# A two-layer network on one core: dummy products, a parameter load and operand casts are placed otherwise

## The chip, the cores and the metric

The kernel runs on one core of a Trainium2 chip. The core has a tensor engine (PE, with its weight loads listed apart as PEld), VectorE (DVE), ScalarE (ACT), GpSimd (POOL) and SyncE (SP), whose queue issues almost all transfers. The metric is the device time of one execution in microseconds (us); three executions before the change took 2072.78, 2072.91 and 2074.65 us, median 2072.91.

## The reference

Two layers on 1024 tokens of 1024 features, float32 throughout. Layer 0 mixes tokens by attention in a sliding window of 128 with a sink, layer 1 by a gated recurrence (HGRN2) in chunks of 64; each is followed by an MLP with a squared ReLU, and every block is preceded by an RMS norm.

```python
for layer in range(DEPTH):
    h = rmsnorm(x, mix_norm[layer])
    y = attention(h, ...) if layer % 2 == 0 else hgrn2_recurrence(h, ...)
    x = x + y
    h = rmsnorm(x, mlp_norm[layer])
    x = x + jnp.square(jax.nn.relu(h @ w_up[layer])) @ w_down[layer]
return rmsnorm(x, final_norm)
```

`rmsnorm` multiplies by the reciprocal root of the mean square over the features and by a gain per feature.

## The kernel before

**Layout.** Activations lie with 128 features on the partitions and 512 tokens along a tile, so a full activation is eight tiles for each of two token halves (`hf`). The program is written as Python code that names operations, their tiles and their costs; it issues nothing itself.

**Products in three parts.** A float32 operand is split in two reduced-precision tiles: `hi`, a cast of it, and `lo`, the operand less `hi`. A product is then three: hi by hi, hi by lo, lo by hi (`mm3`). Weights come from memory into `wr` tiles (or are sums of such tiles, `m`), and `weight_split` makes `wh` and `wl`; for activations `split` does the same. The cast could be placed on ScalarE or on VectorE, whichever suited the plan; the subtraction is always VectorE's. Most large products are arranged after Strassen with seven leaves in place of eight, and three of the leaves of the MLP's up projection again in quarters; of the tile called "4" in those inner leaves only the right half (columns 256 to 511) is read by a product. `pair` makes two of the up projection's 32 blocks of features at a time, 16 pairs a layer; PE accumulates several leaves one after the other in the same bank, and ScalarE copies the bank out between them.

**Order.** All operations go to one planner (`Schedule`). It runs a list of them forward with estimated costs, the engines' queues and buffer releases, and backward for due times, in four passes, and keeps the pass with the earliest end. From this come the order on every engine, the engine of those operations that may choose, and the buffers. At run time each engine works through its own list in that order and waits by semaphores. A changed cost or choice can therefore move instructions anywhere in the program. Line 428 is the helper that issues every operation, so the profile names tiles and not lines: `p` and `q` are banks of the accumulation memory, `a`, `t` and `m` are work tiles, `c` constants, `sm` the few numbers of a norm, `d` memory for tiles put by.

**Start.** `Net.__init__` makes ten products of a zero tile with itself (`warm`), to have the tensor engine active while the first loads come. `first_loads` loads the parameters (gains and lower bounds, 16 rows) by SP's queue, transposes them with four small products into the constant tile `c`, and loads the first activations and weights.

**End.** The down projection's last sum for token half 1 is computed in two parts of 256 tokens. `final` is called three times: for half 0, for the first 256 tokens of half 1, and for the last 256. Each call adds the squares of all features (`sum_squares`), takes the mean over the partitions by products with a column of 1/1024 (`token_rstd`, in two portions, since the last tile of features is finished late), forms the reciprocal root, spreads it over the partitions by products with the identity (`spread`), and multiplies and stores. Between and behind the portions `token_rstd` puts products of the identity with itself, four and five of them, in all three calls. The two calls on 256 tokens spread twice, into two banks, one read by VectorE and one copied by ScalarE for GpSimd.

Of the kernel before, what the change touches and what calls it, by code (L numbers as in the profile page):

```python
# [10 lines left out]
F32 = mybir.dt.float32  # L11
# [3 lines left out]
ALU = mybir.AluOpType  # L15
AX = mybir.AxisListType

P = 128
# [4 lines left out]
TH = T // NH  # L23
# [3 lines left out]
N_PAR = 8 * KT  # L27
# [113 lines left out]
WAIT = 0.5  # L141
TABLE, REUSE, PASSES = 1283.0, 200.0, 4
FULL = {512: 227.3, 256: 119.8}
LEAD = 100
WARM = 10
ROWS = 16
# [4 lines left out]
class Schedule:  # L151
# [40 lines left out]
    def forward(self):  # L192

        free_at, pending, ready, done, form, table = {}, {}, {}, [], None, None
# [179 lines left out]
class Net:  # L374
# [24 lines left out]
    def warm(self, zero, n=WARM, tag="p"):  # L399

        ps = self.psum(tag)
        for _ in range(n):
            self.mm(ps[:, :P], zero, zero, True, True, P, 4)
# [100 lines left out]
    def weight_split(self, z):  # L504
        hi, lo = (self.tile(tag, BUFS[tag], (P, TH), F32R) for tag in ("wh", "wl"))
        self.copy(hi, z, TH, ("ACT", "DVE"), False)
        self.tt("any", lo, z, hi.bitcast(F32), ALU.subtract)
        return hi, lo
# [12 lines left out]
    def split(self, src, new=None):  # L521
        hi, lo = ((new or self.a)(F32R) for _ in range(2))
        self.copy(hi, src, TH, ("ACT", "DVE"), False)
        self.tt("any", lo, src, hi.bitcast(F32), ALU.subtract)
        return hi, lo
# [18 lines left out]
    def token_rstd(self, acc, inner=1.0, outer=1.0, n=TH, keep=False, more=()):  # L544
# [4 lines left out]
        for i, z in enumerate(parts):  # L549
            for j in range(nb):  # L550
                first, last = (j == 0, j == nb - 1) if more else (True, True)
                self.mm(ps[:, j : j + 1], z[:, j * P : j * P + P], self.mean, i == 0 and first, i == len(parts) - 1 and last, P, 2,
                        skip_group_check=bool(more))
            if more and z is acc:
                self.warm(self.ident, 4, "q")
        if more:
            self.warm(self.ident, 5, "q")
# [140 lines left out]
    def strassen_weights(self, first, second, done=(), inner=()):  # L698
# [29 lines left out]
        w = {name: self.weight_split(z) for name, z in order}  # L728
# [3 lines left out]
    def inner_operands(self, own, kept, homes):  # L732
# [33 lines left out]
        for j, c in enumerate((L, R) if homes else ()):  # L766
            hi, lo = part(own[j], R, "R")
            self.copy(hi, t[0][:, c], 2 * P, ("ACT", "DVE"), False)
# [382 lines left out]
    def first_loads(self):  # L1151
# [5 lines left out]
        self.dma(rows[:ROWS], self.io["par"], 4 * P * N_PAR)  # L1157
# [493 lines left out]
    def final(self, hf, tokens=slice(0, TH)):  # L1651
# [3 lines left out]
        y = self.token_rstd(first, n=n, more=[last])  # L1655
        r, rs = self.spread(y, n), self.t()[:, :n]
        self.copy(rs, self.spread(y, n) if n < TH else r, n)
        self.s.lead = -200
        per = TH // n
        for k in range(0, KT, per):  # L1660
# [4 lines left out]
            step = 1 if n < TH and k == per else per  # L1665
# [98 lines left out]
```

## Time and profile before

| | |
|---|---|
| median of three executions | 2072.91 us |
| the profiled execution in all | 2074.11 us |
| its span (first to last instruction) | 2072.3 us |
| records on PE, DVE, ACT, POOL | 12290, 3870, 2319, 121 |
| moved by DMA | 407.44 MB, 197 GB/s on the mean |

A row of the timeline has the start, the duration of the merged row, the engine, the operation, what it writes and reads, the tile, and the count; in brackets stands the idle time ahead of it and what ended it. A row of groups has the busy time in all, the mean duration in ns, and behind the second bar the idle time of that engine just before, with its releasers. Records of successive products overlap, so a product's cost to the stream is the distance between starts. A float32 product of tiles that aren't split shows two records. A row of the windows has the stretch, its length, and then the busy time of PE, PEld, VectorE, ScalarE and GpSimd with their counts. The chain of work that ended last is followed back from the last instruction; its rows have the start, the length and what held the end.

### The profile page before, as it was taken

What the parts mean: (1) busy time and instruction counts of PE and PEld (TensorE: products, weight loads), DVE (VectorE), ACT (ScalarE), POOL (GpSimd) and SP (SyncE); (2) the same over time, 40 slices, a digit from 0 to 9 for tenths busy, and PEclk for the clock granted to TensorE, in tenths of its full rate; (3) what the DMA queues carried; (4) which work ended last, traced back from release to release, by engine and by line L of the source; (5) the groups of instructions that cost most, each with busy time, mean ns of one, the idle gap of its engine ahead of it and who ended that gap; (6) DMA issues with size and microseconds to landing.
All of it is one profiled execution on the core that took longest, in us unless ns stands there. A gap on an engine that the chain in (4) does not pass through costs nothing.

```text
span 2072.3 us, 35730 instructions
## 1 busy us (share of the span) xinstructions
PE 2062.5 (100%) x12290; PEld 1753.2 (85%) x12290; DVE 1908.8 (92%) x3870; ACT 1139.5 (55%) x2319; POOL 61.1 (3%) x121
## 2 busy tenths in 40 slices
PE   9999999999999999999999999999999999999998
PEld 7888788888898888888888888888888888888888
DVE  8999989999999989999999999889999999998994
ACT  7477966655565434656544544444665556433562
POOL 4121000000000000000000000000000000000000
PEclk9999999999999999999999999999999999999999
DMA  6212468777679887542322223677887677996712
GB/s 220 84 45 77 148 229 277 258 242 249 213 243 311 299 262 262 182 129 72 113 102 98 97 93 102 232 245 240 263 265 262 213 241 262 316 311 218 254 51 82
DMA packets 225766, 407.44 MB, mean 197 GB/s; under 512 B 25248, under 2 KB 30368, under 8 KB 225584
## 3 DMA queue, kind: packets, MB, share of 16 engines
q1 hardware_dynamic: 225584, 405.16, 59.2%
q8 instruction: 97, 1.59, 0.3%
q14 instruction: 85, 0.70, 0.1%
HBM read 321.17 MB, written 83.89 MB: 195 GB/s over the span
## 4 chain that ended last, share of the span: by engine, by line
PE 96%; issue 1%; DMA 1%; DVE 1%; ACT 0%; POOL 0%; POOLq 0%; SPq 0%; ACTq 0%
PE p L428 52%; PE q L428 44%; DMA d<-t 0%; ACT t L428 0%; DMA t<-d 0%; DVE t L428 0%; DMA wr<-in_up 0%; DVE m L428 0%; DVE wl L428 0%; DVE a L428 0%; POOL a L428 0%; ACT wh L428 0%; POOLq L1738 0%; ACT a L428 0%; SPq L428 0%
## 5 line engine op out<-in xcount | busy, mean ns | idle before, releaser
L428 PE MATMUL p<-a,wh 128*128 128x512 f32 (+1 forms) x2880 | 804.4, 364 | 0.0
L428 PE MATMUL q<-a,wh 128*128 128x512 f32 x2112 | 653.2, 391 | 1.4 <-ACT t L428 1.4
L428 PEld LDWEIGHTS p<-a,wh 128*128 128x128 f32 x2880 | 515.5, 189 | 84.5 <-issue 0.4
L428 PE MATMUL p<-a,wl 128*128 128x512 f32 (+1 forms) x1440 | 520.4, 362 | 0.0
L428 PEld LDWEIGHTS q<-a,wh 128*128 128x128 f32 x2112 | 389.4, 188 | 78.3 <-ACT t L428 2.8
L428 PE MATMUL q<-a,wl 128*128 128x512 f32 x1056 | 410.2, 389 | 0.0
L428 PEld LDWEIGHTS p<-a,wl 128*128 128x128 f32 x1440 | 271.6, 189 | 40.1
L428 ACT CAST wh<-wr 128x512 fp32r<-128x512 f32 x285 | 175.9, 621 | 182.1 <-PE p L428 138.5
L428 DVE TENSOR_TENSOR wl<-wr,wh 128x512 fp32r<-128x512 f32 x352 | 240.9, 689 | 9.2 <-ACT wh L428 4.6
L428 ACT CAST wh<-m 128x512 fp32r<-128x512 f32 x262 | 162.2, 621 | 152.0 <-PE q L428 78.8
L428 DVE TENSOR_TENSOR wl<-m,wh 128x512 fp32r<-128x512 f32 x338 | 231.2, 689 | 13.1 <-ACT wh L428 4.6
L428 PEld LDWEIGHTS q<-a,wl 128*128 128x128 f32 x1056 | 198.3, 188 | 42.1
L428 DVE TENSOR_TENSOR a<-t,a 128x512 fp32r<-128x512 f32 (+2 forms) x314 | 208.2, 681 | 5.8 <-PE q L428 2.9
L428 DVE TENSOR_TENSOR t<-t,t 128x512 f32<-128x512 f32 (+3 forms) x337 | 197.5, 603 | 10.0 <-ACT t L428 6.9
L428 ACT ACTIVATE t<-t 128x512 f32<-128x512 f32 x228 | 143.7, 632 | 101.6 <-DVE t L428 97.5
L428 ACT COPY t<-q 128x512 f32<-128x512 f32 (+2 forms) x201 | 111.7, 560 | 110.2 <-PE q L428 87.1
L428 ACT CAST a<-t 128x512 fp32r<-128x512 f32 (+1 forms) x206 | 122.6, 610 | 70.7 <-PE q L428 46.6
L428 PE MATMUL p<-wh,a 128*128 128x512 f32 x384 | 125.9, 398 | 1.1 <-ACT a L428 1.1
L428 DVE TENSOR_TENSOR t<-t,p 128x256 f32<-128x256 f32 x294 | 120.8, 417 | 6.0 <-PE p L428 2.1
L428 DVE TENSOR_TENSOR m<-wr,wr 128x512 f32<-128x512 f32 (+1 forms) x188 | 121.5, 648 | 2.6 <-DMA wr<-in_down 1.9
L428 PEld LDWEIGHTS q<-t,t 128*64 128x64 f32 (+1 forms) x2160 | 95.8, 144 | 12.0 <-issue 8.1
L428 PE MATMUL q<-t,t 128*64 128x32 f32 (+2 forms) x2160 | 104.6, 229 | 0.0
(134 smaller groups left out, 2393.0 us busy)
## 6 DMA issues: line engine op xcount, KB each, us to landing
t<-d SPq DMA_DIRECT2D x548, 256.0 KB, 4.2
d<-t SPq DMA_DIRECT2D x244, 256.0 KB, 3.3
wr<-in_down SPq DMA_DIRECT2D x224, 256.0 KB, 4.1
wr<-in_up SPq DMA_DIRECT2D x178, 256.0 KB, 3.7
wr<-in_win SPq DMA_DIRECT2D x68, 256.0 KB, 2.9
a<-d SPq DMA_DIRECT2D x60, 256.0 KB, 4.0
wr<-in_wqkv SPq DMA_DIRECT2D x48, 256.0 KB, 3.1
d<-a SPq DMA_DIRECT2D x48, 256.0 KB, 3.7
```

Source lines behind the costliest of these rows:

```text
L428: fn(*[place(a) for a in args], **{k: place(v) for k, v in kw.items()})
```

## The change

It does six things.

- Of the ten dummy products at the start the count stays, but their cost in the plan is now 430 ns each; the planner also starts its engines at 700 to 850 ns and not at zero (`FIRST`).
- The parameters are loaded by ScalarE's queue and not by SP's.
- `token_rstd` places dummies in the last of the three final calls alone: three and four of them where it had four and five, with a cost of 217 ns in the plan.
- The second spread is made in the last call alone; in the second call one bank is read by both. A group of features that was stored tile by tile in the second and third call is so in the third alone.
- Every cast of a split runs on ScalarE.
- Of the inner leaves' tile "4" only the half that is read is cast and subtracted.

```diff
+FIRST = {"SP": 700.0, "PE": 850.0, "ACT": 700.0, "DVE": 800.0, "Pool": 800.0}
...
-        free_at, pending, ready, done, form, table = {}, {}, {}, [], None, None
+        free_at, pending, ready, done, form, table = dict(FIRST), {}, {}, [], None, None
...
-    def warm(self, zero, n=WARM, tag="p"):
+    def warm(self, zero, n=WARM, tag="p", cost=430.0):
 
         ps = self.psum(tag)
         for _ in range(n):
-            self.mm(ps[:, :P], zero, zero, True, True, P, 4)
+            self.op("PE", self.nc.tensor.matmul, [ps], [zero], cost, ps[:, :P], zero, zero, start=True, stop=True, form="whole")
...
-    def weight_split(self, z):
+    def weight_split(self, z, first=0):
         hi, lo = (self.tile(tag, BUFS[tag], (P, TH), F32R) for tag in ("wh", "wl"))
-        self.copy(hi, z, TH, ("ACT", "DVE"), False)
-        self.tt("any", lo, z, hi.bitcast(F32), ALU.subtract)
+        c, n = slice(first, TH), TH - first
+        self.copy(hi[:, c], z[:, c], n, psum=False)
+        self.tt("any", lo[:, c], z[:, c], hi[:, c].bitcast(F32), ALU.subtract, n)
         return hi, lo
...
     def split(self, src, new=None):
         hi, lo = ((new or self.a)(F32R) for _ in range(2))
-        self.copy(hi, src, TH, ("ACT", "DVE"), False)
+        self.copy(hi, src, TH, psum=False)
...
-    def token_rstd(self, acc, inner=1.0, outer=1.0, n=TH, keep=False, more=()):
+    def token_rstd(self, acc, inner=1.0, outer=1.0, n=TH, keep=False, more=(), busy=(0, 0)):
...
-            if more and z is acc:
-                self.warm(self.ident, 4, "q")
-        if more:
-            self.warm(self.ident, 5, "q")
+            if busy[i > 0]:
+                self.warm(self.ident, busy[i > 0], "q", 217.0)
...
-        w = {name: self.weight_split(z) for name, z in order}
+        w = {name: self.weight_split(z, 2 * P * (isinstance(name, tuple) and name[1] == "4")) for name, z in order}
...
-            self.copy(hi, t[0][:, c], 2 * P, ("ACT", "DVE"), False)
+            self.copy(hi, t[0][:, c], 2 * P, psum=False)
...
-        self.dma(rows[:ROWS], self.io["par"], 4 * P * N_PAR)
+        self.op("ACT", self.nc.scalar.dma_start, [rows], [self.io["par"]], 100, rows[:ROWS], self.io["par"], tail=1800.0)
...
-        y = self.token_rstd(first, n=n, more=[last])
+        ends = n < TH and tokens.stop == TH
+        y = self.token_rstd(first, n=n, more=[last], busy=(3, 4) if ends else (0, 0))
         r, rs = self.spread(y, n), self.t()[:, :n]
-        self.copy(rs, self.spread(y, n) if n < TH else r, n)
+        self.copy(rs, self.spread(y, n) if ends else r, n)
...
-            step = 1 if n < TH and k == per else per
+            step = 1 if ends and k == per else per
```

How the instructions move, at three places. First the tensor engine's list at the very start, before the change and after it; `p_178` is the bank of the dummies, `c_67` the identity, `t_167` and `t_169` the loaded parameters.

```order
L428 MATMUL p_178<-t_169 128x128 x10
L428 MATMUL p_210<-c_67,t_167 128x16 x4
L428 MATMUL p_238<-wh_218,a_226 128x512
L428 MATMUL p_238<-wl_224,a_226 128x512
L428 MATMUL p_244<-wh_218,a_226 128x512
```

```order
L429 MATMUL p_178<-t_171 128x128 x4
L429 MATMUL p_204<-c_67,t_169 128x16 x4
L429 MATMUL p_178<-t_171 128x128 x6
L429 MATMUL p_243<-wh_229,a_233 128x512
L429 MATMUL p_243<-wl_235,a_233 128x512
```

The transposes of the parameters stood behind all ten dummies; now they stand behind four, and six follow them. Next ScalarE's list at the start, before and after; `c_65` is the parameter tile, `a_226` and `a_233` the first scaled activation.

```order
L428 ACT_TABLE_LOAD
L428 COPY c_65<-p_210 128x64
L428 ACTIVATE a_226<-a_194,c_65 128x512
L428 ACTIVATE t_234<-a_194 128x512
L428 ACTIVATE c_230<-c_230 128x8
```

```order
L429 DMA t_169<-in_par 16x512
L429 ACT_TABLE_LOAD
L429 COPY c_65<-p_204 128x64
L429 ACTIVATE c_216<-c_216 128x8
L429 CAST wh_229<-wr_167 128x512
L429 ACTIVATE a_233<-a_184,c_65 128x512
L429 CAST wh_237<-wr_198 128x512
```

The load's issue, a small exponential and the first weights' cast now stand ahead of the first scaled activation. Last the tensor engine's list at the first of the three final calls; `q_24326` and `q_24301` hold the mean, `q_24331` and `q_24340` the dummies, the spread is the row with `sm`, and the `p` rows are products of the down projection's last sum.

```order
L428 MATMUL q_24326<-c_69,t_24144 128x1 x4
L428 MATMUL q_24331<-c_67 128x128 x4
L428 MATMUL q_24326<-c_69,t_23917 128x1 x4
L428 MATMUL q_24340<-c_67 128x128 x5
L428 MATMUL p_21354<-a_24046,a_24035 128x256
L428 MATMUL p_21354<-a_24051,a_24035 128x256
L428 MATMUL p_21354<-a_24046,a_24043 128x256
L428 MATMUL p_21354<-a_24070,a_24059 128x256
L428 MATMUL p_21354<-a_24075,a_24059 128x256
L428 MATMUL q_24360<-c_67,sm_24345 128x128 x4
```

```order
L429 MATMUL q_24301<-c_69,t_24112 128x1 x4
L429 MATMUL q_24301<-c_69,t_23874 128x1 x4
L429 MATMUL p_21331<-a_24013,a_24003 128x256
L429 MATMUL p_21331<-a_24018,a_24003 128x256
...
L429 MATMUL p_21331<-a_24118,a_24096 128x256
L429 MATMUL p_21331<-a_24215,a_24096 128x256
L429 MATMUL q_24333<-c_67,sm_24316 128x128 x4
```

The nine dummies are gone, and fourteen products of the last sum, not five, stand between the mean and its spread. In the second call the same happens, with thirteen products between the two portions of the mean and fourteen more ahead of the spread, which is two products and not four. The third call keeps its place at the end.

## The prediction

> **What bounds the kernel now.** I read the page's busy shares first, then the chain of work that ended last, then what the tensor engine (PE) waited for, and at last the timeline of the start and of the end.
>
> ```profile
> span 2072.3 us, 35730 instructions
> PE 2062.5 (100%) x12290; PEld 1753.2 (85%) x12290; DVE 1908.8 (92%) x3870; ACT 1139.5 (55%) x2319; POOL 61.1 (3%) x121
> PE 96%; issue 1%; DMA 1%; DVE 1%; ACT 0%; POOL 0%; POOLq 0%; SPq 0%; ACTq 0%
> 790.91 43.52 PE p L428 x192
> 1704.23 2.87 PE p L428 x24
> PE q L428 <- ACT t L428: 1.4, 4, 0.4
> PE p L428 <- ACT a L428: 1.1, 1, 1.1
> PE p L428 <- DVE t L428: 1.0, 1, 1.0
> PE q L428 <- DVE sm L428: 0.7, 1, 0.7
> ```
>
> The chain is PE for 96% of the span. Two of its pieces show at what pace: 192 products of 512 columns in 43.52 us are 0.227 us each, 24 of 256 columns in 2.87 us are 0.120 us each, and no group of that kind is slower once the clock is up. The four wait rows are all of PE's idle time, 4.2 us in 2072.3. So VectorE's 92% bounds nothing: whatever it has too much of is hidden ahead of PE. Time comes off here in two ways only, a product that PE no longer executes or a wait of PE that shrinks; and it is lost in one, a new wait of PE.
>
> **The dummy products that go.** They are the products of the identity with itself, `q<-c` with 128 columns; each logical product stands as two records. The timeline of PE at the end:
>
> ```profile
> 2030.34 0.95 PE L428 MATMUL q<-c,t 128*128 128x1 f32 x8
> 2031.15 1.14 PE L428 MATMUL q<-c 128*128 128x128 f32 x8
> 2032.12 0.95 PE L428 MATMUL q<-c,t 128*128 128x1 f32 x8
> 2032.93 1.36 PE L428 MATMUL q<-c 128*128 128x128 f32 x10
> 2034.05 0.83 PE L428 MATMUL p<-a,a 128*128 128x256 f32 x5
> 2034.72 1.05 PE L428 MATMUL q<-c,sm 128*128 128x128 f32 x8
> 2046.89 1.81 PE L428 MATMUL q<-c 128*128 128x128 f32 x14
> 2048.53 0.50 PE L428 MATMUL q<-c,t 128*128 128x1 f32 x4
> 2048.90 0.69 PE L428 MATMUL q<-c 128*128 128x128 f32 x4
> 2049.35 1.44 PE L428 MATMUL p<-a,a 128*128 128x256 f32 x10
> 2050.62 1.05 PE L428 MATMUL q<-c,sm 128*128 128x128 f32 x8
> 2051.43 10.56 PE L428 MATMUL p<-a,a 128*128 128x256 f32 x86
> 2064.20 0.69 PE L428 MATMUL q<-c 128*128 128x128 f32 x4
> 2065.61 1.16 PE L428 MATMUL q<-c,sm 128*128 128x128 f32 x8 [0.72 <-DVE sm L428]
> ```
>
> A duration counts overlapped work, so I take the distance from one row's start to the next one's. First final (tokens of half 0): 2032.12 - 2031.15 = 0.97 and 2034.05 - 2032.93 = 1.12. Second final (first 256 tokens of half 1): 2048.53 - 2046.89 = 1.64 and 2049.35 - 2048.90 = 0.45. Together 4.18 us for 36 records. Was PE waiting in that time anyway? In the new order the 128x256 products of the last sum stand in their place, and their operands don't depend on the norm. What needs time is the chain behind the mean, and its cover is now those products: 14 of them between the mean and the spread of the first final, 14 x 0.120 = 1.7 us, where that chain took at most 34.72 - 32.93 = 1.8 us before; in the second final 14 again, against 50.62 - 48.90 = 1.7 us. The two nearly meet, so a wait of 0.1 us at each is likely the worst; with all of the cover gone it would be 1.7 us at each. I take -4.2. In the third final the two dummies that go (4 records from 2064.20) end before PE's wait of 0.72 us for `sm`: 0.
>
> **The second spread** of the second final: the eight records between 2050.62 and 2051.43 become four, half of 0.81 us: -0.4. The copy for GpSimd then reads the first spread's bank, and VectorE reads the same one; both results are needed 10 us before the last product of that stage ends, so that is hidden. One output transfer fewer changes nothing on PE's path.
>
> **The start.**
>
> ```profile
> 0.73 0.40 SPq L428 DMA_DIRECT2D t<-in_par  x1
> 1.05 4.63 PE L428 MATMUL p<-t 128*128 128x128 f32 x20 [1.05 <-DVE t L428]
> 5.61 0.60 PE L428 MATMUL p<-c,t 16*128 16x16 f32 x4
> 6.25 0.21 ACT L428 COPY c<-p 128x64 f32<-128x64 f32 x1 [4.24 <-PE p L428]
> 6.50 0.72 ACT L428 ACTIVATE a<-a,c 128x512 fp32r<-128x512 f32 x1
> 7.27 0.80 PE L428 MATMUL p<-wh,a 128*128 128x512 f32 x1 [1.06 <-ACT a L428]
> 9.15 1.32 PE L428 MATMUL p<-wh,a 128*128 128x512 f32 x3
> t<-in_par SPq DMA_DIRECT2D x1, 32.0 KB, 1.8
> wr<-in_wqkv SPq DMA_DIRECT2D x48, 256.0 KB, 3.1
> ```
>
> The parameters had landed at 0.73 + 1.8 = 2.5 us, but their transposes stand behind all ten zero products (20 records) and start at 5.61. The new order puts four of the ten ahead (8 records, (5.61 - 1.05) / 20 = 0.23 us each, so until 2.9) and six behind. With the parameters there by 2.9, the transposes run until 3.5, the six others until 3.5 + 12 x 0.23 = 6.2. ScalarE now does more ahead of the first product: copy 0.21, a small exponential that waits for two operations of VectorE, the cast of the weights (0.62, row below) and the scaled copy 0.72; with handovers about 2.5 us from 3.5, also near 6.1. So the first product could start at 6.2 instead of 7.27: -1.1. Against it: the parameters now leave ScalarE's queue while SP sends 256 KB tiles at the same moment. If they land only like such a tile, 0.73 + 3.1 = 3.8, the six dummies end at 7.1: -0.2. Moreover the early products run at about half pace: three from 9.15 on take 1.32 us, 0.44 each against 0.227 later, so what starts earlier there may be work done at the slow pace. I take -0.8, bounds -1.1 and 0; for a loss the parameters would have to land after 4 us. The Trainium skill (Trainium Kernel Development and Optimization, section Key Constraints) says that transfers from SP's, ScalarE's and GpSimd's queues run on the same 16 engines and interleave, so that a second queue only saves issue time; by that rule the parameters share the engines with the first tile and land late, and the sum would be 0.4 us smaller. No row here has two queues at once. The skill's TensorE: Matmul & The Clock Gate (Part 1) says that the window that releases the clock runs freely and doesn't begin with the kernel; by that, an earlier first product may still meet the same release, and this term would shrink to half. One profile can't show that.
>
> **All casts on ScalarE, halves not split.**
>
> ```profile
> L428 ACT CAST wh<-wr 128x512 fp32r<-128x512 f32 x285 | 175.9, 621 | 182.1 <-PE p L428 138.5 <-PE q L428 26.4 <-issue 4.3
> L428 DVE CAST wh<-m 128x512 fp32r<-128x512 f32 x76 | 32.4, 426 | 32.9 <-PE q L428 16.4 <-PE p L428 16.2
> L428 DVE TENSOR_TENSOR wl<-wr,wh 128x512 fp32r<-128x512 f32 x352 | 240.9, 689 | 9.2 <-ACT wh L428 4.6 <-DVE wh L428 0.5
> L428 DVE TENSOR_TENSOR a<-t,a 128x256 fp32r<-128x256 f32 x8 | 3.1, 426 | 0.1
> 200.00:300.00 100.00, 100.00 (x586) 80.49 (x585) 93.54 (x183) 76.14 (x220) 5.98 (x8) 1.00 0.54 176
> 400.00:500.00 100.00, 100.00 (x601) 89.33 (x600) 95.51 (x209) 55.40 (x94) 0.00 (x0) 1.00 0.73 236
> 351.13 1.15 ACT L428 CAST wh<-m 128x512 fp32r<-128x512 f32 x2 [1.99 <-PE q L428]
> 352.18 0.58 ACT L428 COPY t<-q 128x512 f32<-128x512 f32 x1
> ```
>
> Counted over the two orders, 198 casts leave VectorE (198 x 0.426 = 84 us off it) for ScalarE (198 x 0.621 = 123 us on it); 25 squared relus go the other way (25 x 0.689 = 17 us on VectorE, at the price of the `wl` row); 42 splits halve, 689 to 426 ns each, 11 us off VectorE. VectorE ends near 1909 - 84 + 17 - 11 = 1831 us, ScalarE under 1140 + 123 = 1263. None of it is PE's work: 0 directly, covered on both engines by PE's own 100% in the windows (the fourth and fifth column after the sum are VectorE and ScalarE; even the busiest, 200 to 300 us, leaves ScalarE 24%). What it can do is move PE's waits. The four waits "PE q <- ACT t" (1.4 us) are such cases: at 352 ScalarE's copy of a bank that PE wants next stands behind two casts that had waited 1.99 us for PE to free their buffers. A cast is 0.62 us in front of whatever follows it, and nothing overtakes on ScalarE. Copies of a full bank with three or more casts right ahead number 32 in the old order of ScalarE and 63 in the new. Bounds: -1.4, all four waits gone since VectorE is earlier with its part; +1.4, twice as many, if waits go with that count. I take +0.5, a third of the way up, since ScalarE has idle time in every window and the places are planned with its queue in the account.
>
> The other edits (the engines' start times, the dummies' costs) only move places in the plan. I counted PE's switches from products of 64 columns back to full ones in both orders: 41 and 41, so this price is unchanged: 0.
>
> **Sum**: -4.2 - 0.4 - 0.8 + 0.5 = -4.9 us on the profiled span, 2072.3 to 2067.4. That execution took 2074.1 us in all, the three timed ones 2072.78 to 2074.65 with a median of 2072.91; taken off the median: **2068.0**.
>
> **Rivals.** *Given back in small waits.* The dummies and the start bring 5.4 us, and PE's waits behind casts triple: the 1.4 us row taken three times more is +4.2, time 2071.7. For it: 63 against 32; against it: the same planner placed both. *Slower: ScalarE's queue becomes PE's gate.* Place: the pairs of the MLP's up projection, where every pair reads banks through ScalarE and PE writes that bank next. Price: the copy's own 0.58 us at 352, which PE waits out when it comes that late. One such wait in each of the 32 pairs of both layers is +18 us: 2072.9 - 5.4 + 18 = 2085. It decides from 10 waits on, and the 0.2% line is passed at (5.4 + 4.1) / 0.58 = 17. Against it: now there are four in 2072 us, and ScalarE is at 55% there (window 400 to 500). *More than forecast.* The start gains its 1.1 and the four waits vanish: -4.2 - 0.4 - 1.1 - 1.4 = -7.1, 2065.8. *The change doesn't do what it says*, since PE had idled behind the dummies anyway: only 0.8 us at the start, 2072.1. The rows from 2030.34 to 2035 speak against it, they are gapless and products were at hand.
>
> **How the numbers follow.** Forecast 0.60 (its own range 2066.3 to 2069.8), small waits 0.17, no effect 0.04, slower 0.10, more 0.09. A measurement here tells about 0.2%, 4.1 us, from no change; that line is at 2068.8, only 0.8 us above the forecast. Of the forecast's 0.60 some 0.46 lie below it, with "more" 0.55 faster; 0.34 within; 0.11 slower. Two in ten left out, half of it on the slow side: 2064.8 to 2073.0.
>
> **What would show it.** In the profile after: 14 instead of 54 records `q<-c` with 128 columns, PE busy some 4.5 us less, the first `p<-wh,a` at 6.1 to 7.1 us, the last product at about 2062, and the tail of 5.5 us behind it as it was. PE's wait list tells the rest: under 5 us in all is the forecast, 8 the first rival, over 14 the second. It would be wrong if the spread of a final waited for `sm` as long as the dummies had run, or if the first product isn't earlier than 7 us because ScalarE's longer line ahead of it ends last.

## The result and the profile after

The changed kernel takes 2068.07 us (median of 10 executions, 2066.22 to 2068.93), the kernel before, run beside it, 2073.69 us (10 executions, 2072.66 to 2076.43). The ratio is 0.997, 95% interval 0.9961 to 0.998: 5.6 us off, where 4.9 had been forecast from a median that lay 0.8 us lower. That the median meets the forecast 2068.0 to 0.1 us is therefore luck: the higher start and the larger gain cancel. The profiled execution took 2068.05 us.

The page of the changed kernel, its head and the chain of work that ended last:

```profile
span 2066.3 us, 35752 instructions
PE 2056.9 (100%) x12246; PEld 1747.3 (85%) x12246; DVE 1832.5 (89%) x3696; ACT 1202.4 (58%) x2467; POOL 54.8 (3%) x121
PE 96%; issue 2%; DVE 1%; ACT 0%; DMA 0%; POOL 0%; POOLq 0%; ACTq 0%; DVEq 0%
```

PE still carries 96% of the chain. It has 44 records fewer: 40 of dummies, 4 of the spread. VectorE lost 76 us of work and ScalarE gained 63, and neither shows in the span, since both lie beside PE. What PE waited for (engine, what it writes, what it waited for, then us in total, times, the longest):

```profile
PE q L429 <- DVE sm L429: 1.4, 1, 1.4
PE p L429 <- DVE t L429: 1.0, 1, 1.0
PE p L429 <- POOL a L429: 0.7, 1, 0.7
PE q L429 <- ACT t L429: 0.4, 1, 0.4
PE q L429 <- DVE m L429: 0.3, 1, 0.3
```

The four waits for ScalarE's `t` (1.4 us before) are down to one of 0.4. The wait for `sm` has grown from 0.7 to 1.4, and a wait at the start is new. The timeline of PE at the end:

```profile
2028.71 1.84 PE L429 MATMUL q<-c,t 128*128 128x1 f32 x16
2030.41 1.92 PE L429 MATMUL p<-a,a 128*128 128x256 f32 x14
2032.17 1.05 PE L429 MATMUL q<-c,sm 128*128 128x128 f32 x8
...
2045.26 1.91 PE L429 MATMUL p<-a,a 128*128 128x256 f32 x14
2047.01 0.60 PE L429 MATMUL q<-c,sm 128*128 128x128 f32 x4
...
2056.09 1.81 PE L429 MATMUL q<-c 128*128 128x128 f32 x14
2057.74 0.51 PE L429 MATMUL q<-c,t 128*128 128x1 f32 x4
2059.61 1.13 PE L429 MATMUL q<-c,sm 128*128 128x128 f32 x8 [1.36 <-DVE sm L429]
```

Only 14 records `q<-c` are left. The fourteen products of the last sum stand ahead of each of the first two spreads, and no row there has a bracket: PE waits for neither. The third spread waits 1.36 us where it waited 0.72.

The span can now be cut at three rows that both kernels have, the first product of weights, the first row of the first final and the last spread; the rows of before are those of the prediction.

| stretch | before | after | difference | forecast |
|---|---|---|---|---|
| until the first `p<-wh,a` | 7.27 | 6.89 | -0.38 | -0.8 |
| from there to the first final's mean | 2030.34 - 7.27 = 2023.07 | 2028.71 - 6.89 = 2021.82 | -1.25 | +0.5 |
| from there to the last spread | 2065.61 - 2030.34 = 35.27 | 2059.61 - 2028.71 = 30.90 | -4.37 | -4.6 |
| from there to the span's end | 6.7 | 6.7 | 0 | 0 |
| sum | 2072.3 | 2066.3 | -6.0 | -4.9 |

The end came out as forecast. The start brought half of its term, and the middle, for which a small loss had been taken, brought a gain; how firm that gain is, a comparison of five profiles further down shows. The start, on PE and then on ScalarE:

```profile
1.05 2.08 PE L429 MATMUL p<-t 128*128 128x128 f32 x8 [1.05 <-DVE t L429]
3.80 0.57 PE L429 MATMUL p<-c,t 16*128 16x16 f32 x4 [0.68 <-POOL a L429]
4.31 2.93 PE L429 MATMUL p<-t 128*128 128x128 f32 x12
6.89 0.77 PE L429 MATMUL p<-wh,a 128*128 128x512 f32 x1
```

```profile
4.41 0.21 ACT L429 COPY c<-p 128x64 f32<-128x64 f32 x1 [1.96 <-PE p L429]
...
5.68 0.72 ACT L429 ACTIVATE a<-a,c 128x512 fp32r<-128x512 f32 x1
```

And the parameters' transfer in the list of DMA issues (its last number is the time from issue to landing):

```profile
t<-in_par ACTq DMA_DIRECT2D x1, 32.0 KB, 2.9
```

The load was issued at 0.73 us and so landed at 3.63; the transposes start at 3.80. The bracket at 3.80 names GpSimd, but the tile that was missing is the one this load writes (in the kernel with the dummies put back, below, the list puts the same wait down to `DMA t<-in_par`). Behind the transposes the six other dummies run to the end at half pace (2.58 us for 12 records, 0.22 each), and the first product follows them without a gap. ScalarE's line, longer now, ends at 6.4: it was not the gate.

### The profile page after: what moved, and what is told of

Its sections match the earlier page's. It is cut to its first block, busy times and chain, and to the rows that moved or that the text cites. A ratio compares the mean times of both kernels' runs of the same rounds, so it can differ in the third digit from the quotient of the medians.

```text
span 2066.3 us, 35752 instructions
## 1 busy us (share of the span) xinstructions
PE 2056.9 (100%) x12246; PEld 1747.3 (85%) x12246; DVE 1832.5 (89%) x3696; ACT 1202.4 (58%) x2467; POOL 54.8 (3%) x121
## 4 chain that ended last, share of the span: by engine, by line
PE 96%; issue 2%; DVE 1%; ACT 0%; DMA 0%; POOL 0%; POOLq 0%; ACTq 0%; DVEq 0%
PE p L429 52%; PE q L429 44%; DVE a L429 1%; DMA d<-t 0%; DVE m L429 0%; DVE wl L429 0%; DVE t L429 0%; ACT t L429 0%; DVE sm L429 0%; ACT wh L429 0%; POOL t L429 0%; POOL a L429 0%; ACT a L429 0%; POOLq L1739 0%; ACT m L429 0%
## 5 line engine op out<-in xcount | busy, mean ns | idle before, releaser
L429 ACT CAST wh<-m 128x512 fp32r<-128x512 f32 (+1 forms) x338 | 206.3, 613 | 268.8 <-PE q L429 181.8
L429 ACT CAST wh<-wr 128x512 fp32r<-128x512 f32 x352 | 211.7, 603 | 230.1 <-PE p L429 161.5
L429 DVE TENSOR_TENSOR wl<-m,wh 128x512 fp32r<-128x512 f32 (+1 forms) x338 | 226.5, 676 | 49.9 <-ACT wh L429 44.3
L429 DVE TENSOR_TENSOR wl<-wr,wh 128x512 fp32r<-128x512 f32 x352 | 233.5, 666 | 36.1 <-ACT wh L429 35.1
L429 ACT CAST a<-t 128x512 fp32r<-128x512 f32 (+1 forms) x234 | 138.8, 610 | 27.6 <-DVE t L429 10.4
L429 ACT ACTIVATE t<-t 128x512 f32<-128x512 f32 x178 | 112.1, 632 | 73.0 <-DVE t L429 69.8
```

What stands on the lines that cost most here:

```text
L429: fn(*[place(a) for a in args], **{k: place(v) for k, v in kw.items()})
```

## The experiments

All kernels were timed beside the kernel before on the same chip. "Before" differs a little from one group of runs to the next (2073.7 to 2074.3), so the ratio is what compares them; its interval reaches some 2 us either way. The first eight measured the terms one by one and asked whether the gain in the middle is the relief of VectorE by the casts or belongs to the new order; the last four follow from what these showed.

| kernel | median, us | ratio to before, 95% interval |
|---|---|---|
| after | 2068.07 | 0.997 [0.9961, 0.998] |
| before, dummies and spread alone | 2069.52 | 0.998 [0.9971, 0.9989] |
| before, start alone | 2073.88 | 0.9997 [0.9988, 1.0006] |
| before, casts alone | 2073.10 | 0.9995 [0.9986, 1.0003] |
| before, halves alone | 2076.62 | 1.0013 [1.0004, 1.0023] |
| after, dummies back | 2071.10 | 0.9987 [0.9978, 0.9996] |
| after, casts free | 2070.22 | 0.9982 [0.9973, 0.9991] |
| after, parameters by SP | 2069.99 | 0.9978 [0.9969, 0.9987] |
| after, no dummies in the finals | 2067.61 | 0.997 [0.9958, 0.9981] |
| before, store counted 4 us | 2071.49 | 0.9986 [0.9977, 0.9995] |
| before, halves and store 4 us | 2070.64 | 0.9983 [0.9975, 0.9992] |
| before, planned start times alone | 2076.58 | 1.0013 [1.0004, 1.0022] |
| after, three edits more | 2068.43 | 0.9967 [0.9955, 0.998] |

### Dummies and second spread alone, on the kernel before

```diff
-            if more and z is acc:
-                self.warm(self.ident, 4, "q")
-        if more:
-            self.warm(self.ident, 5, "q")
+            if busy[i > 0]:
+                self.warm(self.ident, busy[i > 0], "q")
...
+        y = self.token_rstd(first, n=n, more=[last], busy=(3, 4) if ends else (0, 0))
...
+        self.copy(rs, self.spread(y, n) if ends else r, n)
```

> Before, with the dummies and the second spread for the last tokens alone; the orders of all engines are those of before until the end, so nothing else moves. Theory 1 (PE's own work is the bound, a product that goes comes off whole): span of the profile 4.5 us shorter than before's 2072.3 (4.2 for 36 records, 0.4 for 4 of the spread), so near 2067.8; PE's four waits in mid-kernel (1.4 us) stay. Rival (the dummies stood where PE would have waited for the norm): under 1 us off, and a new wait of PE for sm of 1 to 2 us in each of the first two finals.

Measured 2069.52 beside 2074.33, ratio 0.998. PE's order is that of before until the finals, so what differs is these records. The end in PE's timeline:

```profile
2030.17 1.84 PE L428 MATMUL q<-c,t 128*128 128x1 f32 x16
...
2061.07 1.13 PE L428 MATMUL q<-c,sm 128*128 128x128 f32 x8 [1.37 <-DVE sm L428]
```

From the first final's mean to the last spread it is 30.90 us, to the hundredth what the whole change has there, and the waits in the middle are still in place ("PE q <- ACT t" 1.9 us in five). The dummies' term is shown by itself, and it is most of the result. The ratios 0.998 [0.9971, 0.9989] here and 0.997 [0.9961, 0.998] of the whole change have intervals that overlap: by the times alone it is not shown that the other edits together bring anything.

### The dummies put back into the changed kernel

```diff
-        y = self.token_rstd(first, n=n, more=[last], busy=(3, 4) if ends else (0, 0))
+        y = self.token_rstd(first, n=n, more=[last], busy=(3, 4) if ends else (4, 5))
```

> The changed kernel with four and five dummies back in the first two final calls (18 products, 36 records); the second spread stays out, and the orders are the changed kernel's until the end. Theory 1: 36 x 0.112 to 0.116 us, so 4.0 to 4.2 us longer than the changed kernel's span of 2066.3, at 2070.4. Rival (their time is PE's wait anyway): under 1 us longer.

Measured 2071.1, 0.17% more than the changed kernel by the ratios, or 3.5 us; the span grows by 3.4. The nine dummies of each of the first two calls, 36 records, were 4.18 us by the prediction's rows. From the first final's mean (2028.11) to the last spread (2063.03) it is now 34.92 us where the changed kernel has 30.90, 4.0 us more. The price holds in this direction too.

### No dummies in any final

```diff
-        y = self.token_rstd(first, n=n, more=[last], busy=(3, 4) if ends else (0, 0))
+        y = self.token_rstd(first, n=n, more=[last], busy=(0, 0))
```

> The changed kernel without any dummies in the final calls. Theory 1: the seven dummies of the last call stand where PE waits for ScalarE anyway, and the wait for sm behind them isn't PE's work: 0, within 0.5 us of 2066.3 apart from moved waits. Rival (they keep the clock up for the last spread): the clock falls before the last spread and its products take twice as long, 0.5 us longer.

Measured 2067.61 in 6 executions, ratio 0.997, not to be told from the changed kernel. Of the list of PE's waits, the second row:

```profile
PE q L429 <- ACT t L429: 1.1, 1, 1.1
```

This wait is new (1.08 us at 2056.24, ahead of the last portion of the mean): it stands where the dummies of the last call had run. Their 1.65 us was time in which PE had nothing else for two thirds. The seven that the change keeps are thus worth nothing that the median shows. The rival of the expectation did occur in the profiled execution, though. The last spread:

```profile
2058.21 2.05 PE L429 MATMUL q<-c,sm 128*128 128x128 f32 x8 [1.37 <-DVE sm L429]
```

Its eight records take 2.05 us where they take 1.13 in the changed kernel, the granted clock is 0.50 from 2057 to 2060 us (1.00 from 2057 to 2061 in the changed kernel), and from the start of this spread to the span's end it is 7.6 us, not 6.7. So the seven dummies do not only fill a wait: without them the clock can fall ahead of the last spread. It need not, for in the candidate below, which has no dummies either, the spread takes 1.13 us.

### The start alone

(The planned cost of 217 ns for the dummies of the finals goes with it.)

```diff
+FIRST = {"SP": 700.0, "PE": 850.0, "ACT": 700.0, "DVE": 800.0, "Pool": 800.0}
...
-            self.mm(ps[:, :P], zero, zero, True, True, P, 4)
+            self.op("PE", self.nc.tensor.matmul, [ps], [zero], cost, ps[:, :P], zero, zero, start=True, stop=True, form="whole")
...
-        self.dma(rows[:ROWS], self.io["par"], 4 * P * N_PAR)
+        self.op("ACT", self.nc.scalar.dma_start, [rows], [self.io["par"]], 100, rows[:ROWS], self.io["par"], tail=1800.0)
```

> Before, with the start alone changed: parameters by ScalarE's queue, the planned start times and dummy costs. The casts may still be placed on VectorE. Theory 1 (the transposes come earlier, the six dummies behind them then set the first product): first product between 6.5 and 7.0 us instead of 7.27, and the span 0.3 to 0.6 us shorter apart from waits that the new plan moves (up to 1.5 us either way). Rival (ScalarE's longer list ahead of the first product sets it): with the first cast on VectorE the first product comes earlier than in the changed kernel, before 6.5 us.

Measured 2073.88 beside 2074.33: no difference that can be told, although the first product starts at 6.78 and not at 7.27. The four waits in the middle are gone, with casts still free to go to VectorE, and others of 0.2 to 0.6 us have come in other places.

### The casts alone

```diff
-        self.copy(hi, z, TH, ("ACT", "DVE"), False)
+        self.copy(hi, z, TH, psum=False)
...
-        self.copy(hi, src, TH, ("ACT", "DVE"), False)
+        self.copy(hi, src, TH, psum=False)
...
-            self.copy(hi, t[0][:, c], 2 * P, ("ACT", "DVE"), False)
+            self.copy(hi, t[0][:, c], 2 * P, psum=False)
```

> Before, with all casts on ScalarE and nothing else. Theory 1: PE's work is the same, so the span stays within 1.5 us of 2072.3; which of the small waits stand is chance of the plan. Rival A (VectorE's relief took away PE's four waits): 1 to 2 us shorter, PE's wait list without ScalarE's copies. Rival B (casts in front of copies cost PE): longer by 2 us or more, with more than four waits for ScalarE.

Measured 2073.1, ratio 0.9995: within the noise. The four waits are gone and a longer one has come. The chain of waits there (start, length, what held the end):

```profile
699.11 0.61 ACT wh L428
699.72 0.49 ACT a L428
...
700.26 1.88 PE q L428 x7
```

This is the case that the prediction had described, a bank's copy behind a cast of ScalarE; in the middle of the kernel it happened once, not 32 times.

### The casts free again in the changed kernel

```diff
-        self.copy(hi, src, TH, psum=False)
+        self.copy(hi, src, TH, ("ACT", "DVE"), False)
```

(and the same in the two other places)

> The changed kernel with the casts of the splits free to go to ScalarE or VectorE again. Theory 1: PE's work is the same, the span within 1.5 us of 2066.3. Rival A (the 1 us that came on top was VectorE's relief): 1 to 2 us longer, with PE's waits for ScalarE's copies back, about four of them.

Measured 2070.22, ratio 0.9982; the interval reaches into that of the changed kernel. The four waits did not come back: all waits for ScalarE's `t` sum to 0.2 us. So that these four vanished is not the relief of VectorE by the casts. With the start alone they had vanished as well. The time is another matter. Taken from the twentieth product behind the first one, where PE has its full pace in all five kernels, to the first final's mean:

| kernel | twentieth product | first final's mean | between |
|---|---|---|---|
| before | 13.27 | 2030.34 | 2017.07 |
| before, dummies and spread alone (PE's order still that of before) | 11.93 | 2030.17 | 2018.24 |
| after | 12.99 | 2028.71 | 2015.72 |
| after, dummies back (PE's order still that of after) | 12.89 | 2028.11 | 2015.22 |
| after, casts free | 11.88 | 2029.47 | 2017.59 |

Two executions of the same order of PE differ by 1.2 and by 0.5 us here, so the gain of 1.25 us read from one pair of profiles has the right sign in all pairs but no firm size. With the casts free the stretch is as long as before, and PE has a new wait of 0.70 us at 372 behind a chain of VectorE's work. Whether a part of the middle's gain is VectorE's relief thus stays open.

### The halves alone

```diff
-        self.copy(hi, z, TH, ("ACT", "DVE"), False)
-        self.tt("any", lo, z, hi.bitcast(F32), ALU.subtract)
+        c, n = slice(first, TH), TH - first
+        self.copy(hi[:, c], z[:, c], n, ("ACT", "DVE"), False)
+        self.tt("any", lo[:, c], z[:, c], hi[:, c].bitcast(F32), ALU.subtract, n)
...
-        w = {name: self.weight_split(z) for name, z in order}
+        w = {name: self.weight_split(z, 2 * P * (isinstance(name, tuple) and name[1] == "4")) for name, z in order}
```

> Before, with the unread halves of the inner weights not split. Theory 1: nothing that PE waits for, span within 1 us of 2072.3 apart from waits that the new plan moves. Rival A (VectorE's relief): shorter by 1 us or more, since VectorE has 11 us less in the stretches where the four waits stand (340 to 550 and 1600 us).

A surprise: 2076.62 beside 2074.33, ratio 1.0013, slower, with less work on VectorE and none added anywhere. PE's waits for ScalarE's `t` are 3.7 us in six. The chain at the longest of them:

```profile
428.44 5.79 DMA d<-t
...
434.31 0.59 ACT t L428
...
434.95 1.19 PE q L428 x4
```

No cast stands in it. ScalarE's copy of the bank needs a free tile `t`; the one that the planner gave it is still being stored to memory (`d<-t`), and that store took 5.79 us. The planner counts 2.0 us for a store (`STORE = 2000`). The chains behind the five other waits of this kernel lead to such stores too, of 3.77 to 5.92 us. So I looked at the chains behind the four waits of the kernel before (at 352, 510, 547 and 1604, in this order). In each, one transfer is the longest piece:

```profile
339.81 4.16 DMA d<-t
...
504.12 5.62 DMA t<-d
...
538.99 4.04 DMA wr<-in_up
...
1598.12 5.96 DMA d<-t
```

Two of the four lead to a store: at 1604 the copy that PE waits for had itself waited for it, at 352 the delay comes over work of ScalarE and VectorE. The two others lead to loads, of a tile put by and of weights, which the plan counts with 3.0 us (`LOAD = 3000`). At 547 a store takes part all the same, since a copy of ScalarE had waited 3.38 us for one and ended when the weights landed. All four transfers took longer than the plan counts. In the sums of ScalarE's waits the row for stores is, in the kernel before,

```profile
ACT t L428 <- DMA d<-t: 11.8, 9, 3.4
```

17.2 us with the halves alone, and 2.0 us in the changed kernel. That gave a new theory, that stores land later than the plan counts, and three kernels for it.

### The store counted with 4 us, in the kernel before

```diff
-LOAD, STORE = 3000.0, 2000.0
+LOAD, STORE = 3000.0, 4000.0
```

> The kernel before, with one number changed: the plan that orders every engine's instructions counts 4.0 us for a store of 128x512 where it counted 2.0; no work is added or removed. In the profile of before, nine copies of ScalarE waited 11.8 us for stores d<-t, and four waits of PE, together 8.0 us in the distances between its starts (at 352.0, 509.9, 547.4 and 1604.2 us), stood behind such copies. Theory 'stores land later than the plan counts': with 4.0 us counted the plan gives a copy another tile or another place, ScalarE's list of waits for d<-t falls from 11.8 to under 3 us, PE's waits for ACT t at those places go, and the time is 1.0 to 2.5 us below before: median 2071 to 2073 where before is about 2073.7. Rival 'where waits fall is chance of the plan': the list of d<-t waits falls or not, but PE waits elsewhere by as much, and the time is within 1 us of before.

(The 8.0 us of the expectation is a slip: by the distances between starts the four waits come to 0.57 + 0.37 + 0.55 + 0.50 = 2.0 us; the row of waits has 1.4. That all four stood behind copies waiting for stores is too much as well, by the chains above.) Measured 2071.49, ratio 0.9986, 2.3 us less beside 2073.82. All of PE's waits:

```profile
PE p L428 <- ACT a L428: 1.1, 1, 1.1
PE p L428 <- DVE t L428: 1.0, 1, 1.0
PE q L428 <- DVE sm L428: 0.7, 1, 0.7
```

ScalarE's row for stores is down to 0.3 us in one. Not one wait for ScalarE's `t` is left, and none has come elsewhere. One number in the plan, with no work changed, brings 2.3 us (by the interval 1.0 to 4.8), where the whole change brings 5.6. The waits at 510 and 547 are gone too, although their chains led to loads; so the new order has a part in it that the count for stores doesn't explain.

### The halves, with the store counted with 4 us

The edit of the halves and the one above together.

> The kernel before with the unread halves of weights not split, which alone measured 2076.6 (ratio 1.0013, interval 1.0004 to 1.0023), and the plan's 2.0 us for a store raised to 4.0. Theory 'stores land later than the plan counts': the wait of 1.75 us at 433.1 us and its kin go, ScalarE's waits for d<-t fall from 17.2 to under 4 us, and the time falls by 2.5 to 4.5 us against the halves alone, to 2072 to 2074, not above before. Rival 'chance of the plan': it stays at 2075 or more, or the waits for d<-t go and the time stays.

Measured 2070.64, ratio 0.9983 [0.9975, 0.9992], against 1.0013 [1.0004, 1.0023] for the halves alone: 6 us less, more than expected. By the distances between starts the six waits of the halves alone come to 4.7 us; the rest is not traced. ScalarE's waits for stores fall from 17.2 to 2.0 us, and PE's list is the three rows of the kernel above, with the same numbers. The first product starts at 6.38 here. The executions also lie closer together (2069.23 to 2072.38, against 2073.82 to 2080.94).

### The planned start times alone

```diff
+FIRST = {"SP": 700.0, "PE": 850.0, "ACT": 700.0, "DVE": 800.0, "Pool": 800.0}
...
-        free_at, pending, ready, done, form, table = {}, {}, {}, [], None, None
+        free_at, pending, ready, done, form, table = dict(FIRST), {}, {}, [], None, None
```

> The kernel before with planned start times for the five engines and nothing else: 700 to 850 ns ahead of their first instructions in place of 0, so the plan comes out in another order and no work is changed. Theory 'a new plan moves the waits by itself': PE's waits lie in other places, their sum differs from before by 0.5 to 2 us either way, and the time by as much: median 2071.7 to 2075.7 where before is about 2073.7, with ScalarE's list of waits for d<-t (11.8 us in before) moving the same way as PE's waits for ACT t. Rival 'the waits belong to the kernel's work, not to its order': the four places wait as in before and the time is within 0.4 us of it.

Measured 2076.58, ratio 1.0013 [1.0004, 1.0022]: 2.8 us slower, more than the 0.5 to 2 us expected, with every product, cast and transfer as before; only their order differs. What PE waited for, the first rows:

```profile
PE p L429 <- DVE wh L429: 2.3, 1, 2.3
PE q L429 <- ACT t L429: 1.1, 2, 0.9
```

The first is at the start, where the first weights' cast went to VectorE behind other work; it moves the first product from 7.27 to 7.53. The chain at the longer wait of the second row:

```profile
1491.03 5.10 DMA d<-t
...
1496.74 0.59 ACT t L429
...
1497.37 1.67 PE q L429 x6
```

A store of 5.10 us again. The sum of ScalarE's waits for `d<-t` is small here, 1.4 us, so that sum alone doesn't foretell PE's waits, as the expectation had it: one late store at the wrong place is enough.

### The parameters by SP's queue in the changed kernel

```diff
-        self.op("ACT", self.nc.scalar.dma_start, [rows], [self.io["par"]], 100, rows[:ROWS], self.io["par"], tail=1800.0)
+        self.dma(rows[:ROWS], self.io["par"], 4 * P * N_PAR)
```

> The changed kernel with the parameters first on SP's queue again; the plan, which counts 3 us for such a load, then has seven dummies ahead of the transposes and three behind. Theory 1 (what counts is when the transposes are through and ScalarE's list behind them): the parameters land at 2.5 us, seven dummies end at 4.2, transposes at 4.3, first product near 7.2: 0.3 us later than the changed kernel's 6.89. Rival (ScalarE's queue itself brings the gain): 7.3 or later.

Measured 2069.99, ratio 0.9978, not to be told from the changed kernel. The planner now puts seven dummies ahead of the transposes. The transfer and PE's start:

```profile
t<-in_par SPq DMA_DIRECT2D x1, 32.0 KB, 1.7
```

```profile
1.05 3.36 PE L429 MATMUL p<-t 128*128 128x128 f32 x14 [1.05 <-DVE t L429]
4.34 0.60 PE L429 MATMUL p<-c,t 16*128 16x16 f32 x4
...
6.50 0.80 PE L429 MATMUL p<-wh,a 128*128 128x512 f32 x1
```

First on SP's queue the parameters land after 1.7 us, on ScalarE's after 2.9. The first product starts at 6.50, earlier than the 7.2 of the expectation and than the 6.89 of the changed kernel. So ScalarE's queue brings nothing; what helps at the start is that the transposes no longer stand behind all ten dummies. Yet the time doesn't follow those 0.4 us: the first nine products run here at half pace, some 0.43 us each, and the tenth behind the first starts at 10.74 us where the changed kernel has it at 10.70. The prediction had named this case, that what starts earlier may be work done at the slow pace.

### A candidate: the changed kernel with three edits more

```diff
-LOAD, STORE = 3000.0, 2000.0
+LOAD, STORE = 3000.0, 4000.0
...
+        self.op("SP", self.nc.sync.dma_start, [rows], [self.io["par"]], 450.0, rows[:ROWS], self.io["par"], tail=1800.0)
...
+        y = self.token_rstd(first, n=n, more=[last], busy=(0, 0))
```

> The changed kernel with three further edits: the plan counts 4.0 us for a store; the parameters go first on SP's queue and the plan counts 1.8 us for their landing (4 dummies, the transposes, 6 dummies); no dummies in the final calls. It computes the reference. Theory 'the terms add': the parameters land about 1.1 us earlier and the first product of weights starts at 6.0 to 6.4 us instead of 6.89 (worth 0.3 to 0.5, since the clock's release moves by itself and may take it back or add up to 1.3); no dummies is worth 0 to 0.5; the stores' term 0 to 0.4, since ScalarE waits 2.0 us for stores in the changed kernel. Median 2066.5 to 2067.8, span 2064.9 to 2066.3. Rival 'chance of the plan': new waits of 1 to 2 us in the middle, median 2068 to 2071.

Measured 2068.43 in 5 executions, ratio 0.9967: the same as the changed kernel, above the 2067.8 of "the terms add" and inside the rival's range. The first product starts at 6.17, as expected. PE's list lacks two waits of the changed kernel (0.7 us at the start, 0.4 for ScalarE's `t`), but has two new ones:

```profile
PE q L429 <- DVE t L429: 1.1, 1, 1.1
PE q L429 <- ACT t L429: 1.1, 1, 1.1
```

The second is the one that stands in the place of the last dummies. The first ends at 19.07 us, behind a chain of ScalarE's casts and copies: more than the 0.7 us that PE gains at the start it waits out there. And it costs more than itself. The windows from 20 to 23 us, here and in the changed kernel:

```profile
20.00:23.00 3.00, 3.00 (x9) 2.42 (x9) 2.97 (x18) 0.64 (x3) 0.00 (x0) 0.50 0.69 200
20.00:23.00 3.00, 3.00 (x15) 2.49 (x15) 2.96 (x20) 1.75 (x4) 0.00 (x0) 1.00 0.84 269
```

Behind the wait the granted clock (third from the end) is back at 0.50, and PE has 9 records where it has 15: six products at 0.227 us, an estimated 1.4 us. Whether this happens in each of the five executions (2065.67 to 2069.34 us), one profile does not show. No version run here is shown to beat the changed kernel.

## Why the prediction came out right, step by step

**What bounds the kernel: right.** The differences that could be traced are records of PE that are gone, waits of PE that came or went, and the pace that its clock allows; 76 us off VectorE and 63 us onto ScalarE show nowhere else.

**Dummies, -4.2, and spread, -0.4: right.** The stretch gave -4.37, the same in the kernel with this edit alone, and putting 36 records back cost 4.0 us in that stretch and 3.5 by the ratios. Counting by the distance between starts was the right price. The 0.1 us feared at two spreads did not come: fourteen products covered the chain behind the mean. In the third final the dummies were dropped at no gain, as forecast: the wait for `sm` took over 0.64 us. The seven others there fill a wait of PE; leaving them out changed no median, but in one profile the clock fell ahead of the last spread.

**The start, -0.8: measured -0.38, mis-sized.** The prediction let the parameters be there by 2.9 us and put the case that they land at 3.8, first product at 7.1, only as a bound. They landed at 3.63. The first tile of SP's queue was in flight beside them, and first on SP's queue they took 1.7 us. The Trainium skill's rule (Trainium Kernel Development and Optimization, section Key Constraints), that the queues share the 16 engines and a second queue saves issue time only, speaks for this, and the trace agrees: 2.9 us against 1.7 for the same 32 KB. That ScalarE's queue is slower by itself is not excluded, since no run has it without traffic beside it. That 0.4 us less, which the prediction had worked out beside the rule, is what was measured. Moreover an earlier first product isn't an earlier end: at 6.50 and at 6.17 it brought nothing more, in the first case since the early products ran at half pace.

**Casts and halves, waits of PE, +0.5: measured -1.25 in the stretch, the wrong cause.** The step that failed is the count of bank copies with three or more casts right ahead, 32 against 63, as a measure of the waits. With 63 the waits fell. The runs put another cause in its place: a transfer, most often a store, that takes 3.8 to 6.0 us where the plan counts 2 (or 3 for a load), and behind which a copy of ScalarE and then PE wait. It is shown best for the halves alone: all six waits lead to a store, and with 4 us counted they are gone, and 6 us with them. For the kernel before it is shown for two waits of four; with 4 us counted the waits and 2.3 us go. Two orders are few where a new order alone moved the time by 2.8 us, so the rival that part of both gains is chance of the plan stands. The prediction read the casts ahead of the wait at 352 as waiting for PE; the chain there leads over VectorE's `m` to the store of 4.16 us, and behind its row at 1604 stands the one of 5.96. For the changed kernel the cause is less direct. Its order happens to hold only 2.0 us of such waits, and with the casts free it holds 1.4; no edit in it aims at stores. The one wait for ScalarE's `t` that is left in it, at 1493.9, leads to a store as well:

```profile
1487.80 5.43 DMA d<-t
```

That the four waits went is chance of the new plan, as far as the runs tell, and the size of the middle's gain is not firm.

**The other edits "only move places in the plan: 0": wrong as a rule.** The planned start times alone cost 2.8 us in one order. In the whole change nothing of that can be told apart. A term of 0 ± 3 us would have been honest here, and wider than the -1.4 to +1.4 that was given for the casts.

**Sum.** -4.9 became -6.0 in the profile since the errors partly cancel: the start lacked 0.4, the end 0.2, and the middle brought 1.75 more than forecast. Of the rivals, *more than forecast* describes the middle (the waits vanish) but not the start; *small waits* and ScalarE's queue as PE's gate did not occur, with PE's waits for ScalarE's `t` at 0.4 us in all. Of what the prediction would see in the profile, the 14 records, the first product at 6.89 and waits of PE of 3.8 us in all came; PE is busy 5.6 us less, not 4.5. The single edits, -4.8, -0.5, -1.2 and +2.3 us of the medians, make -4.2, the whole change -5.6; each is uncertain by some 2 us, so whether they add up the runs do not show. Each of them has its own order, and the halves cost only in theirs.

**Left open.** Which tile's reuse in the changed order would wait if a store took 6 us was not tried, nor a planner with the stores' whole spread. Whether the changed kernel's start can be made to pay, past the wait that ends at 19.07 us and the slow clock behind it, is open too, and so is how much of the middle's gain is VectorE's relief.

## What to carry to other kernels

Where one engine has 96% of the chain, its instructions that do nothing are the sure part of an estimate: price them by distances between starts, and see what would run in their place. Where a planner lays out the whole program, give any edit that touches it a term of its own for the waits that move, some 2 to 3 us of 2070 here either way, and don't attribute its sign to the edit until the edit has been run alone and in another order. Follow a wait back past the engine that the row names to the transfer behind it, and compare that transfer's duration in the trace with the one that the plan counts. Do not take the engine's row for the whole way: of four waits that looked alike, two led to stores and two to loads. And look at the clock behind a wait of PE: in two profiles here it fell to 0.50 after PE had waited 1.1 us, while after the 1.6 us of the halves it stayed; a dummy that fills a wait may keep it up.

## What the hardware showed unasked

**Stores of 256 KB.** From issue to landing `d<-t` took 3.3 us on the median (244 of them) and 5.96 in the longest case found behind a wait. The Trainium skill (DMA: Bandwidth & Descriptors, section Anatomy of one DMA) gives, for transfers issued by GpSimd, about 2.0 us and the size over 436 GB/s; by it such a store would take an estimated 2.6 us, and it says that the receipt can take surprisingly long where the target is device memory. These stores go by SP's queue, so the formula is not for them; the measured times are longer, and they decide.

**The clock at the start.** Windows of 2 us at the start of two kernels; each has its busy times, PE first with the count of records, and the granted clock third from the end. The kernel before, then with the dummies' edit alone (the same order on PE until the finals):

```profile
7.00:9.00 2.00, 1.73 (x4) 1.44 (x5) 1.97 (x6) 2.00 (x6) 0.25 (x2) 1.00 0.94 305
9.00:11.00 2.00, 2.00 (x8) 1.53 (x7) 2.00 (x5) 1.09 (x3) 0.00 (x0) 1.00 1.05 400
```

```profile
7.00:9.00 2.00, 1.74 (x8) 1.42 (x9) 1.97 (x6) 2.00 (x6) 0.25 (x2) 1.00 0.88 313
9.00:11.00 2.00, 2.00 (x10) 1.68 (x9) 2.00 (x5) 1.14 (x3) 0.00 (x0) 1.00 1.05 404
```

The two kernels start their first product within 0.01 us of each other (7.27 and 7.26) and run the same list, yet PE ends 12 records in these 4 us in the one and 18 in the other: six products at 0.227 us each, an estimated 1.4 us, come or go with the moment at which the full pace begins. With the casts alone the granted clock is 0.50 from 9 to 11 us, and six records are done there. In the kernel before the granted clock reads 1.00 while the count shows half pace, so at the very start the count is the better witness. The Trainium skill's TensorE: Matmul & The Clock Gate (Part 1) has the window that releases the clock run freely, not from the kernel's start; the trace agrees in so far as the same list reached its full pace at different times. By it, a part of a difference of 1 us between two single profiles can be this phase. That is why the medians of five to eleven executions are compared above.
